# First FFN product of a hybrid encoder step: gate products by VectorE out of PSUM in place, operand sums for the second product by GpSimd

## The chip, the core and the metric

The kernel runs on one core of a Trainium2 chip. A core has a matrix engine (PE in the profile, with its weight loads as PEld), VectorE (DVE), ScalarE (ACT), GpSimd (POOL) and SyncE (SP), which issues most of the DMAs. Every engine works through its own queue in program order and waits at an instruction until the semaphores of that instruction allow it. PE writes its results into PSUM (eight banks of 512 float32 columns on 128 partitions); VectorE and ScalarE read and write PSUM and SBUF; GpSimd works on SBUF here. The metric is the time on the device in microseconds (us); lower is better.

## What is computed

The step runs a two-layer encoder on 1024 prompt frames and 64 sample frames, 1088 columns in all. Layer 0 is an SSD mixer followed by a SwiGLU FFN, layer 1 is band attention followed by a SwiGLU FFN. The change lies in the FFN, which runs once in each layer:

```
def swiglu(u, w_in, w_out):
    g, up = jnp.split(u @ w_in, 2, axis=-1)
    return (jax.nn.silu(g) * up) @ w_out
...
xp = xp + rmsnorm(swiglu(rmsnorm(xp, nw[2]), ffn_w_in[layer], ffn_w_out[layer]), nw[3])
```

The model width is 1024, and the FFN is 2816 wide (22 tiles of 128). Everything is float32; each float32 operand is split into a high part and a low part (`h`, `l_`), and three matmuls (high by high, high by low, low by high) make one product.

## The kernel before

**Layout.** Activations lie transposed: model width on the partitions, frames on the columns. The 1088 columns are cut into two blocks, b=0 with 512 columns and b=1 with 576, and each block into two halves of n=256 or n=288 columns.

**First FFN product.** `back` runs the FFN of one layer. For 6 of the 22 tiles block 0 is computed plainly by `plain_pairs` (`T_PLAIN`): one product for the gate, one for the up part. All other work goes through `run_pair`, which computes gate and up tile of both halves of a block by a scheme of seven products instead of eight (Strassen's in Winograd's form). The products are P1, P6, P2, P7, P5, P4, P3 in this order, each 12 matmuls of 128x128 by 128xn (lines 1389 to 1391). First come 16 pairs with both blocks (`T_BOTH`, tiles k and k+11 in turn for k = 3 to 10), where each product runs for b=0 and then for b=1, except in the very first pair, which runs all of b=0 and then all of b=1; then 6 pairs with block 1 alone (`T_TAIL`: tiles 0, 1, 2, 11, 12, 13). A tile below 11 is called a first-half tile here, and a tile from 11 on a second-half tile (`kh` in `hidden`).

**PSUM.** P1 goes to a bank of a pool of two (`mm`), the other six products take turns on a pool of four banks (`px`). A product can start only when the product four places before it in `px` has been read out. With both blocks, P7 of b=0 takes the bank of P6 of b=0, P5 that of P2, P4 that of P7, P3 that of P5, and the next pair's P6 that of P4. With one block P4 takes the bank of P6, and the next pair's P2 the bank of P5.

**Reading out.** ScalarE copies P1 to `p1` (line 1401). VectorE adds P6 to it as `u2` (1404), P2 into `p1` (1406), and ScalarE takes silu there (1407): the gate of the first half. P7 gives `u3` (1410), P5 gives `c22` and a new `u2` (1413, 1414): `c22` is the up part of the second half. P4 is added into `u3` (1416), ScalarE takes silu (1417), and GpSimd multiplies it by `c22` (1418). P3 is added into `u2` (1420), and GpSimd multiplies `p1` by it into `c22` (1421). For b=1 there is one `p1` buffer, for b=0 there are two; so the copy of P1 of block 1 waits until the multiply of line 1421 of the pair before has read `p1`.

**Operand sums.** `hidden` receives the two finished hidden tiles of a block, stores them to DRAM for the second FFN product (line 1449, issued by SP) and makes the sums that the second product's seven products need (`total`, line 1455): one sum for a first-half tile, three for a second-half tile. All of them run on VectorE. With 22 tiles and 2 blocks in 2 layers that is 176 sums, 24 of them behind `plain_pairs`.

**Weights.** `Weights.pair` prepares the weights of a pair: GpSimd makes two differences (`tt`, lines 317 and 318), VectorE two sums (335, 336), ScalarE and VectorE split them into high and low (371, 372), and GpSimd the low part of the smallest one (`half`, 372). There are three buffers for split weights (`hl`).

**Beside it.** `w2_sums` makes sums of the second product's weights on VectorE (`wsum`, lines 1333 to 1336), tied to PE's progress. In the tail, `loader` and `parted` fetch the first operands of the second product from DRAM and split them on ScalarE and VectorE (lines 1492, 1493).

**What sets the order.** PE's order is written by hand. The other engines' queues are ordered by the scheduler from priorities (`tc.high_priority(HIP)` around everything that reads out a bank) and from its own estimate of times; SP's queue is ordered in the same way.

Of the kernel before, what the change touches and what calls it, by code (L numbers as in the profile page):

```python
# [11 lines left out]
AF = mybir.ActivationFunctionType  # L12
ALU = mybir.AluOpType
# [394 lines left out]
def hybrid_kernel(  # L408
# [5 lines left out]
    V, A, G, PE = nc.vector, nc.scalar, nc.gpsimd, nc.tensor  # L414
# [956 lines left out]
    def run_pair(t_, pr, bs, ends, ops, hid, px, tmp, apart=False, keep=None):  # L1371


        tb = {b: {} for b in bs}
        for (p_, key, c0, i), b in [(x, b) for b in bs for x in PRODS] if apart else [(x, b) for x in PRODS for b in bs]:
            h, v = pr[key]
            n, x = ops[b].n, tb[b]

            def t_new(tag):
                if tag == "u3" and keep is not None:  # L1380
                    return keep[:, t_ * n:(t_ + 1) * n]
                return tmp.tile([P, n], F32, tag=f"{tag}{b}", bufs=2 if tag == "u3" or (tag == "p1" and not b) else 1, name=tag)

            st.wait_for(lambda: i in ops[b].hl)
            ah, al = ops[b].hl[i]
            ps = (px.tile([P, 512], F32, tag="mm", name="px") if p_ != P1 else mm("px"))[:, :n]
            for k in range(4):
                wh, wl = h[:, c0 + k * P:c0 + (k + 1) * P], v[:, c0 + k * P:c0 + (k + 1) * P]
                PE.matmul(ps, wh, ah[:, k, :], start=(k == 0), stop=False)  # L1389
                PE.matmul(ps, wh, al[:, k, :], start=False, stop=False)  # L1390
                at_pe[0] = PE.matmul(ps, wl, ah[:, k, :], start=False, stop=(k == 3))  # L1391
                if k == 1:
                    st.run(6 * n / MMR)
            st.t += 6 * n / MMR
            if b in ends:
                for r in ops[b].rings[i]:
                    r.put()
            with tc.high_priority(HIP):
                if p_ == P1:
                    x["p1"] = t_new("p1")  # L1400
                    A.copy(x["p1"], ps)
                elif p_ == P6:
                    x["u2"] = t_new("u2")
                    V.tensor_tensor(x["u2"], ps, x["p1"], op=ALU.add)  # L1404
                elif p_ == P2:
                    V.tensor_tensor(x["p1"], ps, x["p1"], op=ALU.add)
                    A.activation(x["p1"], x["p1"], AF.Silu)
                elif p_ == P7:
                    x["u3"] = t_new("u3")
                    V.tensor_tensor(x["u3"], ps, x["u2"], op=ALU.add)  # L1410
                elif p_ == P5:
                    x["c22"] = t_new("c22")
                    V.tensor_tensor(x["c22"], ps, x["u3"], op=ALU.add)
                    V.tensor_tensor(x["u2"], ps, x["u2"], op=ALU.add)
                elif p_ == P4:
                    V.tensor_tensor(x["u3"], ps, x["u3"], op=ALU.add)
                    A.activation(x["u3"], x["u3"], AF.Silu)
                    G.tensor_tensor(x["u3"], x["u3"], x["c22"], op=ALU.mult)
                else:
                    V.tensor_tensor(x["u2"], ps, x["u2"], op=ALU.add)  # L1420
                    G.tensor_tensor(x["c22"], x["p1"], x["u2"], op=ALU.mult)
                    hid(t_, b, x["c22"], x["u3"])
            st.pump()
            if p_ in (P2, P7, P4, P3) and b == bs[-1]:
                W.put(p_ == P3)
# [3 lines left out]
    def back(layer, start, cpost, xsrc, xmid, cpre, cpost2, xout, rb_out, done2):  # L1429
# [3 lines left out]
        with ExitStack() as es:  # L1433
# [6 lines left out]
            def hidden(t_, b, x, z, late=None):  # L1440

                kh, k = divmod(t_, KH)
                n = ops[b].n

                def out(i, t):
                    st.spawn(store(i, t), HST)

                def store(i, t):
                    paced(nc.sync.dma_start(hc[:, i, k, HO[b]:HO[b] + n], t))
                    stored[i, b] = stored.get((i, b), 0) + 1  # L1450
                    return
                    yield

                def total(t, x_, y_, op):
                    V.tensor_tensor(t, x_, y_, op=op)
                    return t

                if not kh:
                    s3 = stage[0]()[:, :n] if late is None else late[:, k * n:(k + 1) * n]
                    out(OPI["a11"], x)  # L1460
                    out(OPI["s3"], total(s3, x, z, ALU.subtract))
                    kept[k, b] = z, s3
                    return
                z0, s3 = kept.pop((k, b))
                out(OPI["a12"], x)
                out(OPI["a22"], z)
                out(OPI["s1"], total(z0, z0, z, ALU.add))
                s2 = total(stage[0]()[:, :n], z, s3, ALU.subtract)
                out(OPI["s2"], s2)
                out(OPI["s4"], total(stage[0]()[:, :n], x, s2, ALU.subtract))  # L1470
# [810 lines left out]
```

## Time and profile before

| what | value |
|---|---|
| three runs, us | 2959.5, 2962.66, 2964.96 (median 2962.66) |
| the profiled execution: time and span, us | 2964.38 and 2962.7 |
| TensorE clock granted in it, mean | 0.991 |
| DRAM traffic over the span | 141 GB/s |
| first FFN product with `run_pair`, layer 0 | from about 916 to about 1352 us |
| the same, layer 1 | from about 2280 to about 2717 us |

The page cuts the span into 40 equal slices of 74 us and gives each engine's busy share as a digit in tenths; PEclk is the clock that was granted to TensorE. The two FFNs lie in slices 12 to 21 and 31 to 40.

```profile
PE   8999999999999999999998999999999999999998
DVE  7887878885867776776578778777688777677457
POOL 1333333321022433440021000000131333333012
PEclk9999999999999999999998999999999999999999
```

PE is filled almost everywhere, and GpSimd least. A busy PE can still be a slow PE: the rows for a matmul overlap, and at a lower clock they only become longer.

### The profile page before, as it was taken

To read this page: it belongs to the slowest core of one execution; us is meant where nothing else is said; L and a number is where in the kernel's file an instruction comes from. 1 tells how busy PE (TensorE), PEld (TensorE's weight loads), DVE (VectorE), ACT (ScalarE), POOL (GpSimd) and SP (SyncE) were. 2 spreads that over 40 slices of the span, in tenths; PEclk is the share of its full clock that TensorE was granted. 3 is DMA by queue.
4 is the path that set the end of the run, shared out by engine and by line. 5 is a ranking of instruction groups with operands and counts; after the bars stand their busy time and mean duration, and the time that the engine had idled before them with its cause. 6 is when DMAs were issued, how large, how long until landed. Compare 5 with 4: busy or idle time off the path is not lost. (4 is left out here: it accounts for less than half of the span.)

```text
span 2962.7 us, 58034 instructions
## 1 busy us (share of the span) xinstructions
PE 2864.9 (97%) x22096; PEld 2813.5 (95%) x22096; DVE 2221.4 (75%) x4847; ACT 1367.5 (46%) x2485; POOL 714.1 (24%) x903
## 2 busy tenths in 40 slices
PE   8999999999999999999998999999999999999998
PEld 8999999999999999999997899999999999989998
DVE  7887878885867776776578778777688777677457
ACT  6655545454544222234345566556664222234342
POOL 1333333321022433440021000000131333333012
PEclk9999999999999999999998999999999999999999
DMA  4433333335475454456554222223366445465655
GB/s 137 123 99 100 108 100 106 100 120 179 142 207 145 147 168 156 157 178 214 188 185 148 80 76 78 66 66 91 125 206 190 157 149 166 158 193 183 192 186 166
DMA packets 281479, 424.75 MB, mean 143 GB/s; under 512 B 25328, under 2 KB 231120, under 8 KB 281200
## 3 DMA queue, kind: packets, MB, share of 16 engines
q1 hardware_dynamic: 277968, 410.49, 43.6%
q0 software_dynamic: 3232, 10.56, 2.0%
q8 instruction: 173, 2.83, 0.4%
q14 instruction: 106, 0.87, 0.1%
HBM read 312.30 MB, written 104.19 MB: 141 GB/s over the span
## 5 line engine op out<-in xcount | busy, mean ns | idle before, releaser
L504 PE MATMUL mm<-r,hl 128*128 128x384 f32 (+2 forms) x1704 | 568.3, 334 | 2.7 <-DVE kf L1833 1.2
L506 PE MATMUL mm<-r,hl 128*128 128x384 f32 (+2 forms) x1704 | 551.7, 324 | 5.2 <-DVE hl L385 3.4
L505 PE MATMUL mm<-r,hl 128*128 128x384 f32 (+2 forms) x1704 | 551.3, 324 | 0.0
L1390 PE MATMUL px<-r,hl 128*128 128x288 f32 (+1 forms) x1184 | 350.9, 296 | 0.0
L1389 PE MATMUL px<-r,hl 128*128 128x288 f32 x1056 | 314.9, 298 | 19.3 <-DVE u L1404 8.7
L506 PEld LDWEIGHTS mm<-r,hl 128*128 128x128 f32 x1704 | 322.5, 189 | 6.2 <-DVE hl L385 3.8
L504 PEld LDWEIGHTS mm<-r,hl 128*128 128x128 f32 x1704 | 323.3, 190 | 5.0 <-DVE kf L1833 1.4
L505 PEld LDWEIGHTS mm<-r,hl 128*128 128x128 f32 x1704 | 323.1, 190 | 0.3
L1391 PE MATMUL px<-r,hl 128*128 128x288 f32 x1056 | 314.9, 298 | 0.0
L372 DVE TENSOR_TENSOR hl<-raw,hl 128x1024 fp32r<-128x1024 f32 (+2 forms) x188 | 208.2, 1110 | 141.4 <-ACT hl L371 141.3
L530 POOL TENSOR_TENSOR ssum<-ssum,sq 128x256 f32<-128x256 f32 (+1 forms) x111 | 123.2, 1111 | 573.2 <-ACT sq L529 553.4
L1389 PE MATMUL px<-rx,hl 128*128 128x256 f32 x768 | 217.5, 283 | 24.6 <-DVE u L1404 22.9
L371 ACT CAST hl<-raw 128x1024 fp32r<-128x1024 f32 (+2 forms) x188 | 178.9, 951 | 124.0 <-PE po L1729 86.2
L1390 PEld LDWEIGHTS px<-r,hl 128*128 128x128 f32 x1184 | 225.9, 191 | 0.0
L1389 PEld LDWEIGHTS px<-r,hl 128*128 128x128 f32 x1056 | 201.9, 191 | 22.3 <-DVE u L1404 10.3
L1391 PE MATMUL px<-rx,hl 128*128 128x256 f32 x768 | 214.8, 280 | 3.7 <-DVE hl L372 3.7
L1391 PEld LDWEIGHTS px<-r,hl 128*128 128x128 f32 x1056 | 202.1, 191 | 0.2 <-DVE hl L372 0.2
L1727 PE MATMUL po<-r,hl 128*128 128x288 f32 (+1 forms) x682 | 196.6, 288 | 0.0
L1728 PE MATMUL po<-r,hl 128*128 128x288 f32 (+1 forms) x682 | 196.4, 288 | 0.0
L1729 PE MATMUL po<-r,hl 128*128 128x288 f32 (+1 forms) x682 | 196.4, 288 | 0.0
L1390 PE MATMUL px<-rx,hl 128*128 128x256 f32 x640 | 178.7, 279 | 0.0
L1389 PEld LDWEIGHTS px<-rx,hl 128*128 128x128 f32 x768 | 145.7, 190 | 31.6 <-DVE u L1404 29.9
(433 smaller groups left out, 8301.7 us busy)
## 6 DMA issues: line engine op xcount, KB each, us to landing
raw<-in_w_f_dram SPq DMA_DIRECT2D x104, 512.0 KB, 4.1
wsum<-in_w_f_dram SPq DMA_DIRECT2D x128, 176.0 KB, 3.7
wscr<-wsum SPq DMA_DIRECT2D x128, 176.0 KB, 2.8
raw<-in_w_in_dram SPq DMA_DIRECT2D x40, 512.0 KB, 3.7
MT<-ascr SPq DMA_DIRECT2D x48, 384.0 KB, 4.3
raw<-in_w_so_dram SPq DMA_DIRECT2D x32, 512.0 KB, 4.0
r<-hscr SPq DMA_DIRECT2D x22, 576.0 KB, 5.5
raw<-in_w_o_dram SPq DMA_DIRECT2D x19, 512.0 KB, 3.6
```

The source lines that it names most:

```text
L371: self.nc.scalar.copy(h, v)
L372: (eng or self.eng or self.nc.vector).tensor_tensor(lo, v, h, op=ALU.subtract)
L504: PE.matmul(ps[:, :n], h_, xh, start=(first and i == 0), stop=False)
L505: PE.matmul(ps[:, :n], h_, xl, start=False, stop=False)
L506: PE.matmul(ps[:, :n], l_, xh, start=False, stop=(last and i == nk - 1))
L530: (eng or G).tensor_tensor(ssum[:, :n], ssum[:, :n], q[:, :n], op=ALU.add)
L1389: PE.matmul(ps, wh, ah[:, k, :], start=(k == 0), stop=False)
L1390: PE.matmul(ps, wh, al[:, k, :], start=False, stop=False)
L1391: at_pe[0] = PE.matmul(ps, wl, ah[:, k, :], start=False, stop=(k == 3))
L1727: PE.matmul(ps[:, :n], wh, xh, start=(k == 0), stop=False)
L1728: PE.matmul(ps[:, :n], wh, xl, start=False, stop=False)
L1729: at_pe[0] = PE.matmul(ps[:, :n], wl, xh, start=False, stop=(k == KH - 1))
```

## The change

Three things change in `run_pair` and `hidden`:

- P4 is added to `u3` in its PSUM bank, silu is taken in the bank, and VectorE, no longer GpSimd, multiplies the bank by `c22` into `u3`.
- P3 is added to `u2` in its bank, and VectorE multiplies the bank by `p1` into `c22`.
- The sums of `hidden` (line 1455) run on GpSimd, no longer on VectorE.

```
                 elif p_ == P4:
-                    V.tensor_tensor(x["u3"], ps, x["u3"], op=ALU.add)
-                    A.activation(x["u3"], x["u3"], AF.Silu)
-                    G.tensor_tensor(x["u3"], x["u3"], x["c22"], op=ALU.mult)
+                    V.tensor_tensor(ps, ps, x["u3"], op=ALU.add)
+                    A.activation(ps, ps, AF.Silu)
+                    V.tensor_tensor(x["u3"], ps, x["c22"], op=ALU.mult)
                 else:
-                    V.tensor_tensor(x["u2"], ps, x["u2"], op=ALU.add)
-                    G.tensor_tensor(x["c22"], x["p1"], x["u2"], op=ALU.mult)
+                    V.tensor_tensor(ps, ps, x["u2"], op=ALU.add)
+                    V.tensor_tensor(x["c22"], ps, x["p1"], op=ALU.mult)
                     hid(t_, b, x["c22"], x["u3"])
...
                 def total(t, x_, y_, op):
-                    V.tensor_tensor(t, x_, y_, op=op)
+                    G.tensor_tensor(t, x_, y_, op=op)
                     return t
```

The scheduler then orders the queues anew. PE's queue stays as it was. Three places matter below.

VectorE, end of the first second-half pair with both blocks in layer 0 (tile 14), before the change; `px` is a PSUM bank, `sg` and the `u` with another number on both sides are operand sums:

```order
L335 TENSOR_TENSOR tt<-tt,raw 128x512
L1416 TENSOR_TENSOR u_11608<-px,u_11608 128x256
L1455 TENSOR_TENSOR u_11300<-u_11300,u_11608 128x256
L1455 TENSOR_TENSOR sg<-u_11608,sg 128x256
L1416 TENSOR_TENSOR u_11623<-px,u_11623 128x288
L372 TENSOR_TENSOR hl<-tt,hl 128x1024
L1420 TENSOR_TENSOR u_11539<-px,u_11539 128x256
L1455 TENSOR_TENSOR u_11422<-u_11422,u_11623 128x288
L336 TENSOR_TENSOR tt<-raw,tt 128x512
L1455 TENSOR_TENSOR sg<-c_11653,sg 128x256
L1420 TENSOR_TENSOR u_11556<-px,u_11556 128x288
L1455 TENSOR_TENSOR sg<-u_11623,sg 128x288
```

After one more sum of the same kind come the four `wsum` sums and then line 1404 of the next pair. The same place after the change:

```order
L335 TENSOR_TENSOR tt<-tt,raw 128x512
L1416 TENSOR_TENSOR px<-px,u_11608 128x256
L1418 TENSOR_TENSOR u_11608<-px,c_11653 128x256
L1416 TENSOR_TENSOR px<-px,u_11623 128x288
L372 TENSOR_TENSOR hl<-tt,hl 128x1024
L1418 TENSOR_TENSOR u_11623<-px,c_11669 128x288
L1420 TENSOR_TENSOR px<-px,u_11539 128x256
L336 TENSOR_TENSOR tt<-raw,tt 128x512
L1421 TENSOR_TENSOR c_11653<-px,p_11505 128x256
L1420 TENSOR_TENSOR px<-px,u_11556 128x288
L1421 TENSOR_TENSOR c_11669<-px,p_11524 128x288
L1333 TENSOR_TENSOR wsum<-wsum 128x352
```

The six sums are gone, four multiplies have come in; the first multiply stands straight behind the add whose silu it needs, and the four `wsum` sums and line 1404 follow as before.

GpSimd at the same place, before:

```order
L317 TENSOR_TENSOR tt<-raw 128x512
L1418 TENSOR_TENSOR u_11608<-u_11608,c_11653 128x256
L1418 TENSOR_TENSOR u_11623<-u_11623,c_11669 128x288
L318 TENSOR_TENSOR tt<-raw 128x512
L1421 TENSOR_TENSOR c_11653<-p_11505,u_11539 128x256
L372 TENSOR_TENSOR half<-raw,half 128x512
L1421 TENSOR_TENSOR c_11669<-p_11524,u_11556 128x288
```

And after:

```order
L317 TENSOR_TENSOR tt<-raw 128x512
L1455 TENSOR_TENSOR u_11300<-u_11300,u_11608 128x256
L1455 TENSOR_TENSOR sg<-u_11608,sg 128x256
L318 TENSOR_TENSOR tt<-raw 128x512
L1455 TENSOR_TENSOR u_11422<-u_11422,u_11623 128x288
L372 TENSOR_TENSOR half<-raw,half 128x512
L1455 TENSOR_TENSOR sg<-c_11653,sg 128x256
L1455 TENSOR_TENSOR sg<-u_11623,sg 128x288
L1455 TENSOR_TENSOR sg<-c_11669,sg 128x288
```

Four multiplies have become six sums, two of them ahead of the weights' difference of line 318. In a first-half pair GpSimd has the lines 317, 318 and 372 first and then two sums.

VectorE in the first pair of the tail of layer 0 (tile 0, block 1 alone), before; line 1493 splits operands of the second product:

```order
L335 TENSOR_TENSOR tt<-tt,raw 128x512
L1493 TENSOR_TENSOR rx<-rx 128x1024 x2
L1413 TENSOR_TENSOR c_15595<-px,rx 128x288
L1414 TENSOR_TENSOR u_15527<-px,u_15527 128x288
L1416 TENSOR_TENSOR rx<-px,rx 128x288
L1420 TENSOR_TENSOR u_15527<-px,u_15527 128x288
L1493 TENSOR_TENSOR rx<-rx 128x768
L1455 TENSOR_TENSOR rx<-c_15595,rx 128x288
L1404 TENSOR_TENSOR u_15676<-px,p_15661 128x288
L372 TENSOR_TENSOR hl<-tt,hl 128x1024
```

And after:

```order
L335 TENSOR_TENSOR tt<-tt,raw 128x512
L1416 TENSOR_TENSOR px<-px,rx 128x288
L1493 TENSOR_TENSOR rx<-rx 128x1024
L1413 TENSOR_TENSOR c_15595<-px,rx 128x288
L1414 TENSOR_TENSOR u_15527<-px,u_15527 128x288
L1418 TENSOR_TENSOR rx<-px,c_15595 128x288
L1420 TENSOR_TENSOR px<-px,u_15527 128x288
L1493 TENSOR_TENSOR rx<-rx 128x1024
L1421 TENSOR_TENSOR c_15595<-px,p_15508 128x288
L1493 TENSOR_TENSOR rx<-rx 128x768
L1404 TENSOR_TENSOR u_15676<-px,p_15661 128x288
L372 TENSOR_TENSOR hl<-tt,hl 128x1024
```

One split now stands ahead of line 1414 instead of two, and three stand ahead of line 372 as before.

## The prediction

> **What bounds the kernel now.** I read the page first, then PE's waits. The page's first part shows each engine's busy time:
>
> ```profile
> PE 2864.9 (97%) x22096; PEld 2813.5 (95%) x22096; DVE 2221.4 (75%) x4847; ACT 1367.5 (46%) x2485; POOL 714.1 (24%) x903
> ```
>
> PE is the bound, so the change is worth what it takes from PE's waits, and nothing else. The view of waits, PE alone, lists them by who ended them:
>
> ```profile
> PE px L1389 <- DVE u L1404: 31.6, 33, 2.4
> ...
> PE px L1389 <- DVE u L1414: 6.1, 2, 3.0
> PE px L1389 <- DVE u L1410: 4.0, 2, 3.0
> ```
>
> All three are a product of `run_pair` that waits for its bank to be read out by VectorE: 41.7 us, the largest sum in the whole list. Why is VectorE late? The timeline of VectorE at the end of the pair of tile 14 tells it (start, duration, instruction, idle before):
>
> ```profile
> 968.98 1.23 DVE L336 TENSOR_TENSOR tt<-raw,tt 128x512 f32<-128x512 f32 x1
> 970.13 1.51 DVE L1455 TENSOR_TENSOR sg<-c,sg 128x256 f32<-128x256 f32 x1
> ...
> 973.07 0.46 DVE L1455 TENSOR_TENSOR sg<-c,sg 128x288 f32<-128x288 f32 x1 [0.70 <-POOL c L1421]
> 973.45 0.52 DVE L1333 TENSOR_TENSOR wsum<-wsum 128x352 f32<-128x352 f32 x1
> ...
> 975.56 0.79 DVE L1404 TENSOR_TENSOR u<-px,p 128x256 f32<-128x256 f32 x2
> ```
>
> GpSimd and PE in the same stretch:
>
> ```profile
> 960.91 1.28 POOL L317 TENSOR_TENSOR tt<-raw 128x512 f32<-128x512 f32 x1 [9.97 <-DMA raw<-in_w_f_dram]
> 963.79 0.73 POOL L1418 TENSOR_TENSOR u<-u,c 128x256 f32<-128x256 f32 x1 [1.59 <-ACT u L1417]
> ...
> 967.45 1.29 POOL L318 TENSOR_TENSOR tt<-raw 128x512 f32<-128x512 f32 x1
> 968.70 0.95 POOL L1421 TENSOR_TENSOR c<-p,u 128x256 f32<-128x256 f32 x1
> 969.62 1.74 POOL L372 TENSOR_TENSOR half<-raw,half 128x512 fp32r<-128x512 f32 x1
> 972.14 0.90 POOL L1421 TENSOR_TENSOR c<-p,u 128x288 f32<-128x288 f32 x1 [0.78 <-POOL half L372]
> ```
>
> ```profile
> 974.79 0.29 PE L1391 MATMUL px<-r,hl 128*128 128x288 f32 x1
> 976.03 0.39 PE L1389 MATMUL px<-rx,hl 128*128 128x256 f32 x1 [0.95 <-DVE u L1404]
> ```
>
> GpSimd ends the pair's last multiply at 973.04, because a weight difference of 1.74 us stands ahead of it. VectorE's last sum waits for that; four `wsum` sums follow (973.45 to 975.56), then line 1404, whose first half frees the bank at about 975.98. PE was ready at 975.08. Over the pairs with both blocks, VectorE's own waits name the same cause:
>
> ```profile
> DVE sg L1455 <- POOL c L1421: 28.6, 23, 2.0
> ```
>
> A long wait costs more than itself. Two of them in PE's timeline, and then the windows behind the five longest, with the granted clock in the third column from the right:
>
> ```profile
> 1291.75 0.61 PE L1389 MATMUL px<-r,hl 128*128 128x288 f32 x1 [3.04 <-DVE u L1414]
> 1335.85 0.61 PE L1389 MATMUL px<-r,hl 128*128 128x288 f32 x1 [2.43 <-DVE u L1404]
> ```
>
> ```profile
> 1292.00:1298.00 6.00, 6.00 (x26) 6.00 (x27) 4.43 (x8) 2.27 (x5) 3.18 (x3) 0.50 0.70 242
> 1336.00:1340.00 4.00, 4.00 (x21) 4.00 (x22) 4.00 (x6) 2.21 (x3) 0.00 (x0) 0.63 0.33 87
> 2656.00:2662.00 6.00, 6.00 (x34) 5.81 (x34) 4.43 (x8) 2.49 (x5) 3.15 (x3) 0.72 0.57 181
> 2700.00:2704.00 4.00, 4.00 (x20) 4.00 (x21) 4.00 (x6) 2.33 (x3) 0.00 (x0) 0.60 0.38 103
> 2297.00:2303.00 6.00, 5.49 (x30) 5.50 (x31) 3.43 (x9) 0.90 (x2) 1.47 (x2) 0.72 0.67 210
> ```
>
> What is missing to 1.0 is lost: 6x0.50 + 4x0.37 + 6x0.28 + 4x0.40 + 6x0.28 = 9.4 us. The ceiling of the gain from these waits is 41.7 + 9.4 = 51.1 us.
>
> **The multiplies.** GpSimd loses 152 of them (lines 1418, 1421) and VectorE gets them:
>
> ```profile
> L1418 POOL TENSOR_TENSOR u<-u,c 128x288 f32<-128x288 f32 x18 | 23.8, 1322 | 27.4 <-ACT u L1417 27.4
> L1421 POOL TENSOR_TENSOR c<-p,u 128x288 f32<-128x288 f32 x21 | 18.2, 866 | 11.9 <-POOL half L372 11.7
> L1420 DVE TENSOR_TENSOR u<-px,u 128x288 f32<-128x288 f32 x21 | 9.4, 446 | 0.0
> ```
>
> One bank operand and one SBUF operand take VectorE 446 ns, against 866 to 1322 on GpSimd. No row here has VectorE write a bank; its nearest rows are line 1420 (446 ns) and the longest sum below (1533 ns), and I take 0.45. Even at 1.5 VectorE has room: with both blocks it is busy 238 of 337 us (the row below), and per layer 76 multiplies at 0.45 are 34 us while 76 sums leave it.
>
> ```profile
> 935.00:1272.00 337.00, 325.28 (x2589) 321.76 (x2588) 238.41 (x415) 92.16 (x156) 122.75 (x107) 1.00 0.50 161
> ```
>
> The multiply of line 1418 adds a wait: VectorE stands still from the end of the add until ScalarE's silu is done. Queued behind it are the next block's add, a weight split and line 1420. The silu costs:
>
> ```profile
> L371 ACT CAST hl<-tt 128x1024 fp32r<-128x1024 f32 x42 | 43.8, 1042 | 20.2 <-PE px L1391 20.1
> ...
> L1417 ACT ACTIVATE u<-u 128x288 f32<-128x288 f32 x18 | 8.0, 443 | 12.1 <-DVE u L1416 12.1
> ```
>
> ScalarE already waits for that add, so the stall is about 0.5 us, once per pair with both blocks (for block 1 the split of 1.2 us covers it). Bounds: 0.4, and 1.5 when a cast of 1.04 us is in ScalarE's way. The bank of P4 is held for 0.9 us longer (silu and multiply), that of P3 for 0.45; each has four products until its next use, and a product of 12 matmuls takes 12 x 337/2589 = 1.56 us, so over 5 us: no cost.
>
> **The sums.** VectorE loses 176, GpSimd gets them. Here they took:
>
> ```profile
> L1455 DVE TENSOR_TENSOR u<-u,u 128x288 f32<-128x288 f32 x8 | 12.3, 1533 | 2.9 <-POOL u L1418 2.9
> L1455 DVE TENSOR_TENSOR sg<-c,u 128x288 f32<-128x288 f32 x8 | 3.7, 458 | 8.8 <-POOL c L1421 8.8
> ```
>
> The same work takes 458 ns, or 1533 where a GpSimd instruction runs beside it. Line 1420, with one SBUF input, shows no such spread. The page SBUF — State Buffer of the Trainium skill (Who interferes with whom) has a rule that speaks against this change: a VectorE instruction with two SBUF inputs and a GpSimd instruction that reads SBUF exclude each other for their whole length, so each sum moved to GpSimd can hold up the weight splits and `wsum` sums that stay on VectorE. The two rows agree with it; what it would make of the time is the first rival.
>
> On GpSimd I take 0.85 us a sum (line 1421; bounds 0.73 and 1.5), so six are 5.1 us in place of four multiplies of some 4 us; a pair of 14 products lasts 14 x 1.56 = 22 us, so GpSimd keeps room.
>
> **Pairs with both blocks.** In the pair above, the first multiply can begin when GpSimd's did, at 963.79, and ends at about 964.2. Two sums, 1.7 to 3.0 us, then line 318 (1.29) give 967.2 to 968.5; before it was 968.74. Then VectorE: line 336 1.23, lines 1421, 1420, 1421 1.3, four `wsum` sums 2.1, line 1404 0.42, together 5.1 us: the bank is free between 972.3 and 973.6, and PE needs it at 975.1. The slack is 1.5 to 2.8 us. In first-half pairs no sum stands ahead of line 318, so the slack is larger. The waits for line 1404 end in these pairs.
>
> **The first pair.** Line 1410 waits for a buffer whose store follows a sum:
>
> ```profile
> 923.02 0.42 DVE L1363 TENSOR_TENSOR x<-mmx,x 128x256 f32<-128x256 f32 x1
> ...
> 926.09 1.66 DVE L336 TENSOR_TENSOR tt<-raw,tt 128x512 f32<-128x512 f32 x1
> ...
> 933.78 0.42 DVE L1410 TENSOR_TENSOR u<-px,u 128x256 f32<-128x256 f32 x1 [4.57 <-DMA hscr<-x]
> ```
>
> VectorE made that sum only behind the weight sum of line 336, so after 927.75. Its inputs were there at 923.44 (line 1363), and on GpSimd nothing but a DMA issue stands ahead, so the store leaves some 4 us earlier and the 4.0 us of PE waits go.
>
> **The tail.** The 3.0 us wait for line 1414 comes from two splits ahead of it:
>
> ```profile
> 1287.54 3.42 DVE L1493 TENSOR_TENSOR rx<-rx 128x1024 fp32r<-128x1024 f32 x2
> 1290.88 0.45 DVE L1413 TENSOR_TENSOR c<-px,rx 128x288 f32<-128x288 f32 x1
> ...
> 1295.66 1.22 DVE L372 TENSOR_TENSOR hl<-tt,hl 128x1024 fp32r<-128x1024 f32 x1
> ```
>
> After, one split stands ahead, and VectorE arrives 2.2 us earlier: it has lost two sums of 1.53 and two of 0.46 and gained four multiplies of 0.45. From 1285.3 an add, one split (1.2 to 2.3) and two read-outs free P5's bank at 1287.9 to 1289.0. PE wanted it at 1288.7, and without two waits of the mean 0.96 (31.6/33) ahead of it at 1286.8: 1 to 2 us are left. Behind it two splits (2.1 to 3.2), four read-outs and multiplies (1.8) and the weight split itself (1.22 at 1295.66 before) still follow, 5.1 to 6.2 us, which ends at 1293 to 1295; PE wants these weights two products after its wait, at 1291.7: 1.5 to 3.5 us. I take 4 us a layer for both. The wait of 2.43 at 1335.85 loses two sums of 1.53 and one of 0.46 from its chain: nothing is left of it.
>
> New waits: 2 x 4 = 8 us. With the clock that they cost, by the rows of 0.50 to 0.72 about 1 us each, 2 us more. By the page TensorE: Matmul & The Clock Gate of the Trainium skill (Part 1) the clock falls only after an idle window of about 3.4 us, so these waits would cost nothing more and the gain were 43.1; the wait of 2.43 us with 0.63 behind it says otherwise.
>
> **The sum.** 51.1 - 8 - 2 = 41.1 us. The profiled execution took 2964.38 us (span 2962.7), which gives 2923.3; it lies 1.7 above the median of 2962.66, from which I get 2921.6, rounded 2922.
>
> **The rivals.**
>
> *Half.* GpSimd's sums run while VectorE does the `wsum` sums and weight splits, all with two SBUF inputs. In second-half pairs three sums meet four `wsum` sums. One that did so took 1.13:
>
> ```profile
> 1279.17 1.13 DVE L1333 TENSOR_TENSOR wsum<-wsum 128x352 f32<-128x352 f32 x1
> ```
>
> If each of the four does, 2.4 us are added, and up to 1 us on the splits: more than the slack of 1.5. For: the 1533 ns row. Against: GpSimd was busy there before, too. Price: a wait of about 1.4 us in the 16 second-half pairs, 22 us: 2944. This is what the rule of the Trainium skill's page SBUF — State Buffer comes to here.
>
> *No gain.* The stall at silu and the longer banks take the place of the waits, one for one. Over 44 pairs 41.1 us is 0.9 us each, on top of the slack of 1.5: VectorE would have to lose 2.4 us in each; the worst bound of the stall is 1.5. 2963.
>
> *Slower.* Place: line 318 behind two sums. If line 318 comes later than 967.2 by more than 2.8 us, every us beyond is PE's; over 16 second-half pairs it eats the 41.1 us at 2.6 us more, so it decides from 5.4 us of lateness. GpSimd's raw weights arriving late (its 9.97 us wait before line 317 in this pair) plus sums at 1.5 could do it. At 7 us: 16 x 4.2 = 67, less 41.1, gives 2989. Against: the multiplies stood at the same place before.
>
> *More.* The tail's new waits do not come: 2962.7 - 51.1 = 2912. VectorE also has 12 sums less a layer around the first pair, 12 x 0.46 = 5.5 us, of which half may reach PE: 2906.
>
> **How the numbers follow.** Forecast (gain 30 to 51) 0.61, half 0.18, more 0.07, no gain 0.06, slower 0.08. The range takes in the first three: 2906 to 2950 (half with a bad tail), leaving out about 0.17. Faster by over 0.2% (5.9 us, about what a measurement of this kernel tells from no change) 0.86, within 0.06, slower 0.08.
>
> **What would show it.** Right: PE's waits for line 1404 fall from 31.6 to under 5 us, the one for 1410 goes, VectorE's waits for GpSimd's line 1421 are gone, and in the tail PE waits for line 372. Half: rows of `wsum` near 1.1 us and waits for 1404 in every second pair. Wrong: VectorE's wait for line 318, or for silu, in microseconds per pair.

## The result and the profile after

The changed kernel takes 2917.52 us (median of 4 runs, 2915.51 to 2922.25), beside 2963.81 us for the kernel before on the same chip: ratio 0.9847, 95% interval 0.983 to 0.9865. That is 46 us less, where the prediction had 41 (2922, range 2906 to 2950). The profiled execution has a span of 2916.6 us, 46.1 less than before.

The first part of the page after:

```profile
PE 2850.9 (98%) x22096; PEld 2806.7 (96%) x22096; DVE 2237.3 (77%) x4823; ACT 1367.2 (47%) x2485; POOL 753.1 (26%) x927
```

VectorE and GpSimd are both busier than before (2221.4 and 714.1 us), and the kernel is faster. The view of waits, PE alone, its largest lines for products of `run_pair` (line waited for: us in total, times, longest):

```profile
PE px L1391 <- DVE hl L372: 5.9, 5, 2.4
PE px L1389 <- DVE u L1414: 4.7, 3, 2.5
PE px L1389 <- DVE u L1410: 2.8, 1, 2.8
```

Four more lines, 1363, 1406, 371 and 1418, have one wait each, 1.9 us together. Of the 5.9 us for line 372, 5.6 lie in the first pairs and only 0.3 in a tail. Line 1404, 31.6 us in 33 waits before, is gone. VectorE's own waits show why: no line is left in which it waits for GpSimd's line 1421, nor for any multiply or sum. It waits for silu, as expected, and longer than before for stores:

```profile
DVE u L1418 <- ACT px L1417: 13.0, 30, 0.4
DVE c L1413 <- DMA hscr<-c: 10.4, 7, 2.8
DVE u L1410 <- DMA hscr<-x: 8.7, 2, 6.3
```

VectorE at the end of the pair of tile 14, the place that the prediction worked through:

```profile
965.33 1.78 DVE L336 TENSOR_TENSOR tt<-raw,tt 128x512 f32<-128x512 f32 x1
...
967.85 0.46 DVE L1421 TENSOR_TENSOR c<-px,p 128x288 f32<-128x288 f32 x1
968.22 1.18 DVE L1333 TENSOR_TENSOR wsum<-wsum 128x352 f32<-128x352 f32 x1
...
971.47 1.01 DVE L1336 TENSOR_TENSOR wsum<-wsum 128x352 f32<-128x352 f32 x1
972.40 0.78 DVE L1404 TENSOR_TENSOR u<-px,p 128x256 f32<-128x256 f32 x2
```

GpSimd and PE there:

```profile
965.27 1.29 POOL L318 TENSOR_TENSOR tt<-raw 128x512 f32<-128x512 f32 x1
...
968.98 1.02 POOL L1455 TENSOR_TENSOR sg<-c,sg 128x256 f32<-128x256 f32 x1
...
971.13 0.97 POOL L1455 TENSOR_TENSOR sg<-c,sg 128x288 f32<-128x288 f32 x1
```

```profile
973.95 0.28 PE L1389 MATMUL px<-rx,hl 128*128 128x256 f32 x1
```

Three sums run on GpSimd beside the four `wsum` sums, and these last from 968.22 to 972.48, 4.26 us, where they took 2.11 before. The sign of the rival *Half* is there in full, but its price is not: line 1404's first half ends at 972.81 and PE takes the bank at 973.95, without a wait. 1.14 us of room are left.

### The profile page after: what moved, and what is told of

It is laid out like the page before. It is cut to its first block, busy times and chain, and to the rows that moved or that the text cites. A ratio compares the mean times of both kernels' runs of the same rounds, so it can differ in the third digit from the quotient of the medians.

```text
span 2916.6 us, 57887 instructions
## 1 busy us (share of the span) xinstructions
PE 2850.9 (98%) x22096; PEld 2806.7 (96%) x22096; DVE 2237.3 (77%) x4823; ACT 1367.2 (47%) x2485; POOL 753.1 (26%) x927
## 4 chain that ended last, share of the span: by engine, by line
PE 81%; DVE 10%; DMA 4%; ACT 2%; issue 2%; SPq 0%; POOL 0%; DVEq 0%; ACTq 0%; POOLq 0%
PE px L1390 8%; PE px L1391 8%; PE px L1389 8%; PE mm L504 8%; PE mm L506 8%; PE mm L505 8%; PE po L1729 4%; PE po L1728 4%; PE po L1727 4%; PE mmx L505 3%; PE mmx L506 3%; PE mmx L504 3%; PE ptp L1955 2%; PE po L1990 2%; PE S L1924 1%
## 5 line engine op out<-in xcount | busy, mean ns | idle before, releaser
L372 DVE TENSOR_TENSOR hl<-raw,hl 128x1024 fp32r<-128x1024 f32 (+2 forms) x188 | 214.1, 1141 | 125.5 <-ACT hl L371 125.4
```

The lines of the kernel that those rows point to most:

```text
L372: (eng or self.eng or self.nc.vector).tensor_tensor(lo, v, h, op=ALU.subtract)
```

## The experiments

Each kernel was timed beside the kernel before on one chip; ratios are against that. Where times lie close, I also give the length of the two stages (first to last matmul of lines 1389 to 1391, both layers together): 871.1 us before, 826.8 after. What lies between the stages is untouched, yet it differs between profiles by up to 7 us (923.9 to 930.9). Every edit also makes the scheduler order the queues anew, so a run shows a move together with its new order.

**Which of the moves makes the gain?** First the multiplies alone, then the sums alone:

```diff
 def total(t, x_, y_, op):
-    G.tensor_tensor(t, x_, y_, op=op)
+    V.tensor_tensor(t, x_, y_, op=op)
```

> Half of the change: the multiplies of lines 1418 and 1421 on VectorE out of the banks, the sums of line 1455 left on VectorE. My theory (the waits came from VectorE's last sum waiting for GpSimd's multiply; after the change the pairs that hold second-half tiles have 0.8 to 1.3 us to spare at line 1404, the others 1.8 to 2.8): VectorE's waits for GpSimd's line 1421 (55.5 us before) are gone, and the wsum sums are back at 0.52 us (from 1.1) because GpSimd does no sums beside them, which gives 2.1 us back per second-half pair; but six sums of 0.46 to 1.5 us now stand ahead of them, 2.8 us and more. Net some 1 to 2 us later than in the changed kernel, against 0.8 to 1.3 to spare: waits of 0 to 1 us for line 1404 in the 16 to 22 second-half pairs, none in the others: 2918 + 0 to 20, I say 2928. Rival (taking the multiplies off GpSimd is the whole gain, where the sums run does not matter): 2918, no waits for line 1404.

Measured: 2912.44 us, ratio 0.983 (0.9815 to 0.9845), stages 825.0. That is all of the gain, and my theory was too dark by 16 us. VectorE in the same pair, and the product of PE that takes the bank:

```profile
966.11 0.51 DVE L1333 TENSOR_TENSOR wsum<-wsum 128x352 f32<-128x352 f32 x1
...
966.91 0.51 DVE L1334 TENSOR_TENSOR wsum<-wsum 128x352 f32<-128x352 f32 x1
967.35 0.68 DVE L336 TENSOR_TENSOR tt<-raw,tt 128x512 f32<-128x512 f32 x1
967.95 0.51 DVE L1335 TENSOR_TENSOR wsum<-wsum 128x352 f32<-128x352 f32 x1
968.39 0.41 DVE L1404 TENSOR_TENSOR u<-px,p 128x256 f32<-128x256 f32 x1
```

```profile
971.35 0.28 PE L1389 MATMUL px<-rx,hl 128*128 128x256 f32 x1
```

The room is 971.35 - 968.80 = 2.55 us, more than with the sums on GpSimd; 0.51 of it comes from the order, since line 1404 now stands ahead of the last `wsum` sum. VectorE makes six sums more, but with GpSimd quiet its `wsum` sums fall back to 0.51 us and line 336 to 0.68. Two windows of the same length in the stage with both blocks (here, then the changed kernel; behind the window's length stand the busy times of PE, weight loads, VectorE, ScalarE and GpSimd, then the granted clock) show that moving the sums off VectorE freed nothing on it, 244.3 us against 247.9:

```profile
935.00:1255.00 320.00, 320.00 (x2574) 320.00 (x2574) 244.30 (x471) 93.64 (x156) 64.99 (x46) 1.00 0.52 168
```

```profile
935.00:1255.00 320.00, 320.00 (x2574) 320.00 (x2573) 247.90 (x415) 91.66 (x155) 124.96 (x104) 1.00 0.52 170
```

The sums alone, with the multiplies on GpSimd as before:

> The other half: the sums of line 1455 on GpSimd, the multiplies left on GpSimd as before. My theory: VectorE no longer waits for GpSimd (wait for line 1421 gone), but GpSimd's last multiply is now behind three or four sums of about 1 us, so it ends 3 to 4 us later than before; ScalarE's copy of line 1401 for the second block waits for it (it has one p1 buffer), and line 1404 for that copy. The wait moves from VectorE's sum to ScalarE's copy and is of the same size: PE's waits for line 1404 10 to 40 us, time 2945 (2925 to 2970). Rival (the waits came from VectorE standing at the sum and from nothing else): no waits for line 1404 above 5 us in all, 2918 to 2922.

Measured: 3018.2 us, ratio 1.0188 (1.0171 to 1.0205): 56 us slower, and 48 us above the end of the range that my theory gave. The move of the sums is a loss by itself. PE's waits, VectorE's and ScalarE's:

```profile
PE px L1389 <- DVE u L1404: 66.8, 36, 6.2
```

```profile
DVE tt L335 <- POOL tt L317: 96.8, 41, 5.1
DVE u L1404 <- ACT p L1401: 95.8, 41, 3.8
```

```profile
ACT p L1401 <- POOL c L1421: 290.9, 41, 10.0
```

The copy of line 1401 waits as expected (192.1 us in 41 waits before), but it is not all. GpSimd and SyncE in this kernel, from the pair of tile 14 on:

```profile
973.92 1.28 POOL L372 TENSOR_TENSOR half<-raw,half 128x512 fp32r<-128x512 f32 x1
...
988.20 1.29 POOL L317 TENSOR_TENSOR tt<-raw 128x512 f32<-128x512 f32 x1 [11.35 <-DMA raw<-in_w_f_dram]
```

```profile
975.24 0.33 SPq L279 DMA_DIRECT2D raw<-in_w_f_dram  x1
```

The half split ends at 975.20 (971.36 before). It is the last reader of a weight buffer, so SyncE issues the next weight load right behind it, and everything of the next pair's weights comes some 4 us later: line 335 begins at 989.53, before at 985.41. This I had not named, and it hits the first-half pairs, which I had called safe: in layer 0 the eight of them end in 15.3 us of waits for line 1404, the eight second-half pairs in 12.9.

**Which multiply?** From the kernel with the multiplies moved and the sums left, line 1418 goes back to GpSimd (with silu and add in SBUF), or line 1421 does:

```diff
-V.tensor_tensor(ps, ps, x["u3"], op=ALU.add)
-A.activation(ps, ps, AF.Silu)
-V.tensor_tensor(x["u3"], ps, x["c22"], op=ALU.mult)
+V.tensor_tensor(x["u3"], ps, x["u3"], op=ALU.add)
+A.activation(x["u3"], x["u3"], AF.Silu)
+G.tensor_tensor(x["u3"], x["u3"], x["c22"], op=ALU.mult)
```

> One of the two multiplies alone: line 1421 (product P3, the last of a pair) on VectorE out of the bank; line 1418 stays on GpSimd, the sums on VectorE. With both multiplies moved and the sums left, the time was 2912 and line 1404 had 2.5 to 2.9 us to spare. Theory A (what was late is GpSimd's last multiply of a pair, line 1421, as the prediction has it): with it gone nearly all of the gain is there. VectorE's sum behind line 1418 still waits up to 1.3 us and line 318 comes about 1.3 us later, which the room covers: 2912 to 2922, I say 2916, under 8 us of waits for line 1404. Theory B (each hand-over between VectorE and GpSimd in a pair costs its share): about half, 2937, 15 us of waits.

```diff
-V.tensor_tensor(ps, ps, x["u2"], op=ALU.add)
-V.tensor_tensor(x["c22"], ps, x["p1"], op=ALU.mult)
+V.tensor_tensor(x["u2"], ps, x["u2"], op=ALU.add)
+G.tensor_tensor(x["c22"], x["p1"], x["u2"], op=ALU.mult)
```

> The other multiply alone: line 1418 (product P4, with silu in the bank) on VectorE; line 1421 stays on GpSimd, behind line 318 and half a weight split, the sums on VectorE. Theory A (line 1421 being behind the half split is the cause): VectorE's waits for GpSimd's line 1421 stay, and with them most of PE's waits for line 1404: 20 to 30 us of them, 2945 to 2960. Theory B (each hand-over has its share): without line 1418, GpSimd comes to line 318 several us sooner, its last multiply ends some 2 to 4 us sooner, and 1 to 1.5 us of room are left at line 1404: 2914 to 2925, I say 2920. I hold B for the likelier one for this run.

Measured: line 1421 alone 2922.43, ratio 0.9861 (0.9843 to 0.9879), stages 830.8; line 1418 alone 2934.37, ratio 0.9899 (0.9877 to 0.9921), stages 845.8. So the last multiply of the pair is worth 39 us of the 50 by itself, at the upper end of what theory A had, with 2.2 us of waits for line 1404 left, all in the tails. But line 1418 by itself is worth 27, which neither theory gave: A had 2945 to 2960, and B, which I held for the likelier one, 2914 to 2925. GpSimd, without line 1418, comes to its last multiply sooner (in the pair of tile 14 it ends at 971.71, before at 973.04). The two overlap. With line 1418 alone moved, VectorE's sums into `sg` keep 32.5 of the 55.5 us that they waited for line 1421 over both layers before, and little room is left:

```profile
DVE sg L1455 <- POOL c L1421: 32.5, 48, 2.0
```

```profile
PE px L1389 <- DVE u L1404: 8.7, 9, 1.7
```

**What is the bank worth?** Both multiplies on VectorE with two SBUF inputs, silu and adds in SBUF as before. First with the sums on GpSimd, then with the sums on VectorE:

```diff
-G.tensor_tensor(x["u3"], x["u3"], x["c22"], op=ALU.mult)
+V.tensor_tensor(x["u3"], x["u3"], x["c22"], op=ALU.mult)
-G.tensor_tensor(x["c22"], x["p1"], x["u2"], op=ALU.mult)
+V.tensor_tensor(x["c22"], x["p1"], x["u2"], op=ALU.mult)
```

> The change without the banks: both multiplies on VectorE and the sums on GpSimd, but line 1416 and line 1420 write to SBUF as before, silu stays in SBUF, and the multiplies have two SBUF inputs. My theory (VectorE instructions with two SBUF inputs and GpSimd's sums hold each other up, those with a bank input don't): the rows of lines 1418 and 1421, 0.44 us and never over 0.46 in the changed kernel, show means of 0.55 to 0.9 with longest ones over 1 us; GpSimd's sums beside them get slower too; some 0.5 to 1.5 us of VectorE time per pair, against 0.8 to 1.3 to spare in second-half pairs: 2918 to 2930, I say 2922. Rival (the place of the operand does not matter): rows of 0.45, 2918.

> Only the engine of both multiplies is changed: they run on VectorE with two SBUF inputs, silu and both adds stay in SBUF as before, the sums stay on VectorE. Against the run with the same sums and the multiplies out of the banks (2912), it shows what the banks are worth while GpSimd does no sums. Theory (two SBUF inputs cost only where a GpSimd instruction runs beside them; with the sums on GpSimd line 1421 took 1.03 us that way and the time was 2930): GpSimd is quiet but for line 318 and the half split, so the row of line 1421 shows 0.45 to 0.75 us, and the room of 2.5 to 2.9 us covers it: 2912 to 2917, no waits for line 1404. Rival (the bank is worth its 12 us in itself, by freeing or reading it): 2924 or more.

Measured: 2929.82, ratio 0.9888 (0.9873 to 0.9902), stages 842.5, with the sums on GpSimd; 2918.1, ratio 0.9845 (0.9825 to 0.9865), stages 828.0, with the sums on VectorE. The row of line 1421 in the changed kernel, then in these two (shortest, median and longest of its instructions, in ns):

```profile
L1421 DVE TENSOR_TENSOR c<-px,p x76: 409/445/459, 936.5 to 2673.5; 128x288 f32<-128x288 f32 x44, 128x256 f32<-128x256 f32 x32
```

```profile
L1421 DVE TENSOR_TENSOR c<-p,u x76: 426/1028/1571, 934.2 to 2684.4; 128x288 f32<-128x288 f32 x44, 128x256 f32<-128x256 f32 x32
```

```profile
L1421 DVE TENSOR_TENSOR c<-p,u x76: 425/451/1570, 932.1 to 2672.5; 128x288 f32<-128x288 f32 x44, 128x256 f32<-128x256 f32 x32
```

Out of the bank no instruction of 76 took over 0.46 us, though 72 of them ran beside a GpSimd instruction. From SBUF it takes that only where GpSimd is quiet: in the last of these kernels 38 of the 76 ran beside a GpSimd instruction, and 36 of these took over 0.6 us; none of the other 38 took over 0.455. The bank is worth 12 us in the kernel with the sums on GpSimd; with the sums on VectorE a worth between 0 and 5 us cannot be told from nothing, since the intervals of 0.9845 and 0.983 overlap.

**How much room is there at line 1404?** In the changed kernel, the last multiply of each pair made five times:

```diff
-V.tensor_tensor(x["c22"], ps, x["p1"], op=ALU.mult)
+for _ in range(5 if b == bs[-1] else 1):
+    V.tensor_tensor(x["c22"], ps, x["p1"], op=ALU.mult)
```

> The changed kernel with the last multiply of each pair (line 1421 of its last block) made five times, 4 x 0.45 = 1.8 us of VectorE more ahead of the wsum sums and line 1404. It measures the room at line 1404. Theory (the contention took 2.1 us of a room of 3 in second-half pairs and left 0.8 to 1.3; 1.8 to 2.8 in first-half pairs): waits for line 1404 of 0.5 to 1.0 us come back in some 16 to 22 second-half pairs, none in the first-half ones: 12 to 20 us of waits, time 2932. Rival (the room is wider than that, since VectorE was idle at other points and catches up): under 5 us of waits, under 2924.

Measured: 2955.52, ratio 0.9973 (0.9962 to 0.9985). It did not measure what it was made for. The repeats were interleaved with the `wsum` sums, the last of which fell behind line 1404, and in the pairs with both blocks PE hardly waits (0.9 us for line 1404 in layer 0, 1.0 in layer 1). The time was lost in the tails, where the five multiplies, with weight splits between them, held the bank of product P3 for 6 us longer (the loop makes the code a line longer, so line 1422 is this multiply):

```profile
PE px L1389 <- DVE c L1422: 28.1, 8, 5.8
```

What it does show: a bank held some 6 us longer is no longer free of cost. The 0.45 and 0.9 us of the change cost PE one wait of 0.4 us (line 1418). The room at line 1404 stays unmeasured.

**The tail.** A second buffer for c22 of the second block, in the changed kernel:

```diff
-bufs=2 if tag == "u3" or (tag == "p1" and not b) else 1
+bufs=2 if tag == "u3" or (tag == "c22" and b) or (tag == "p1" and not b) else 1
```

> The changed kernel with a second buffer for c22 of the second block. In the changed kernel's tail VectorE stands at line 1413 until the store of an earlier c has landed (10.4 us in 7 waits, 3.9 in 2 before), because that store left SyncE behind stores of sums that GpSimd had not made yet; PE then waits for line 1414 (4.7 us). Theory (the store behind GpSimd's sums is what ends the tail's wait): VectorE's waits for stores of c fall from 10.4 to under 2 us, PE's for line 1414 from 4.7 to under 2, with the clock 3 to 5 us in all: 2913. Rival (VectorE arrives at that place late anyway, for the splits of line 1493): PE's wait for line 1414 or for line 372 stays at 4 us or more, 2917.

Measured: 2916.01, ratio 0.9838 (0.9818 to 0.9858), stages 824.8. VectorE's waits for stores of c are gone, and PE's for line 1414 fall from 4.7 to 0.2. But line 372 takes their place, 2.5 us in the first tail and 2.4 in the second:

```profile
PE px L1391 <- DVE hl L372: 10.1, 6, 2.5
```

The theory was right about the store and wrong about the time. With the store's wait gone, a wait of the same size stands behind the three splits of line 1493 that VectorE makes ahead of line 372, as the rival had it.

**The first pair.** In the changed kernel, two of the last tile's three sums of the first stage go back to VectorE; only s1, for whose store I took line 1410 to wait, stays on GpSimd:

```diff
-def total(t, x_, y_, op):
-    G.tensor_tensor(t, x_, y_, op=op)
+def total(t, x_, y_, op, last=False):
+    (V if last and not b and t_ == T_PLAIN[-1] else G).tensor_tensor(t, x_, y_, op=op)
...
-s2 = total(stage[0]()[:, :n], z, s3, ALU.subtract)
+s2 = total(stage[0]()[:, :n], z, s3, ALU.subtract, True)
...
-out(OPI["s4"], total(stage[0]()[:, :n], x, s2, ALU.subtract))
+out(OPI["s4"], total(stage[0]()[:, :n], x, s2, ALU.subtract, True))
```

> The changed kernel with two of the three sums of the last tile of the first stage back on VectorE; the one whose store line 1410 waits for stays on GpSimd. Theory (three sums of 1.4 to 1.7 us each on GpSimd hold up line 318 there, SyncE's weight load waits for line 318, and the store stands behind that load): the load leaves some 2 us sooner, VectorE's waits at line 1410 for a store fall from 8.7 to under 6 us, PE's from 2.8 to under 1: 2914. Rival (the store's own landing or VectorE's splits end that wait): 2.8 us stay, 2917.

Measured: 2916.11, ratio 0.9843 (0.9822 to 0.9865), stages 822.6. VectorE's wait at line 1410 for the store falls from 8.7 to 5.1 us, as expected, PE's only from 2.8 to 2.4 (1.5 and 0.9 in the two layers), where I had expected under 1. The stages are 4 us shorter, but that is the clock: PE's waits in them are 15.7 us, 15.3 in the changed kernel, while the granted clock was 1.00 where there it was 0.93 for 26 us (2255 to 2281) and 0.72 for 6 us (from 2615). The whole time cannot be told from the changed kernel's.

**A faster kernel?** The multiplies out of the banks, all sums on VectorE but that one; and the same with a split of the tail on GpSimd:

```diff
-out(OPI["s1"], total(z0, z0, z, ALU.add))
+out(OPI["s1"], total(z0, z0, z, ALU.add, G if not b and t_ == T_PLAIN[-1] else V))
```

> A try at a faster kernel, and a test of the first pair: both multiplies on VectorE out of the banks, all sums on VectorE but one, the sum of the last tile of the first stage whose store line 1410 of the first pair waits for; that one is on GpSimd. Theory (on VectorE that sum stands behind weight splits, in the second layer until 2264.9, while SyncE is ready for its store at 2259.9; on GpSimd it is done 7 us sooner and ahead of line 318, so neither line 318 nor SyncE's queue is held up; with all three sums of that tile on GpSimd, as in the changed kernel, line 318 came 2 us late, SyncE's weight load waited for it, and the stores stood behind that load): PE's wait for line 1410 in the second layer (2.4 us) goes, in the first layer it stays, since there the store's landing ends it: 2.5 to 4.5 us less than with all sums on VectorE, 2909. Rival (the transfer is slow because of the four weight loads beside it, whenever it starts): the waits stay, 2912.

```diff
-paced(V.tensor_tensor(rr(l_), l_, rr(h_), op=ALU.subtract))
+paced((G if (p_, b) == USE[0] and k == 4 else V).tensor_tensor(rr(l_), l_, rr(h_), op=ALU.subtract))
```

> A try at a faster kernel: both multiplies on VectorE out of the banks, all sums on VectorE but the one of the first pair (its run was 2912), and the second of the three splits of line 1493 in each tail on GpSimd, which is idle there. Theory (in the tail PE waits 2.1 us a layer for line 372, and VectorE makes that split 1.2 us behind one of line 1493 of 1.2 to 2.3 us): the two waits fall below 1 us each, 3 to 5 us less: 2908. Rival (on GpSimd the split takes 2.5 us and more, beside VectorE's own two-input splits, and holds up the half split of line 372): the waits move to the half split's product or stay: 2912.

Measured: the first 2912.54, ratio 0.983 (0.9809 to 0.9852), with the shortest stages of all, 819.7; PE's wait for line 1410 is down to 0.3 us over both layers, where I had expected it to stay in the first; yet the time is the rival's 2912, not 2909. The second 2914.99, ratio 0.9834 (0.9815 to 0.9854), stages 821.6: its waits in the tails moved back from line 372 to line 1414 (2.1 and 2.9 us). The rival was right here, by VectorE's sum of line 335, which took 0.69 us in the first tail of the changed kernel (at 1269.42). VectorE, then GpSimd:

```profile
1267.20 2.88 DVE L335 TENSOR_TENSOR tt<-tt,raw 128x512 f32<-128x512 f32 x1 [1.43 <-POOL tt L317]
```

```profile
1267.12 2.41 POOL L1493 TENSOR_TENSOR rx<-rx 128x1024 fp32r<-128x1024 f32 x1
```

Neither is proved faster than the plain move of the multiplies.

**The changed kernel again:**

> The changed kernel itself, unaltered, beside the three above on the same chip. It is to say how much of the 5 us between it (2917.5) and the kernel with the sums left on VectorE (2912.4) is its own spread: the two stages that the change touches differ by 1.8 us only in the two profiles (826.8 against 825.0 us), the rest lies in stretches that neither touches. If the sums on GpSimd do cost 5 us, this run comes out at 2916 to 2919; if the difference is spread, at 2911 to 2915.

Measured: 2918.47, ratio 0.9845 (0.9825 to 0.9866), stages 827.5. Both times that it was run, the changed kernel came out 5 to 6 us above the two kernels with the sums left on VectorE (2912.44, 2912.54), 4 to 5 by the ratios. All these intervals overlap, so I take it as likely, not shown, that the sums on GpSimd cost some 5 us. The traces don't show where: PE's waits in the stages are 15.3 and 15.6 us in the two profiles of the changed kernel, and 15.5 with all sums on VectorE.

## Why the prediction was right, step by step

**The bound and the cause.** Right. PE's waits for line 1404 went from 31.6 us to nothing, with VectorE's waits for line 1421. That the multiplies did it is shown by the first two experiments; the prediction had counted sums and multiplies as one move, and so credited the sums with a part that they do not have.

**The multiplies.** 0.45 us was right (409 to 459 ns), the silu stall too: 13.0 us in 30 waits, 0.43 each, against 0.5. The longer hold of the banks cost next to nothing, one wait of 0.4 us.

**The sums.** 0.85 us was too low: the changed kernel's medians by operands lie between 0.81 and 1.72 us, and nine of the ten are 0.95 or more. That VectorE gains what its sums leave free was wrong: in the window above it is 3.6 us busier with them gone. The `wsum` sums show it best, in the changed kernel and with the sums on VectorE: medians of 1.146 and 0.510 us. The rule of the Trainium skill's page SBUF — State Buffer (Who interferes with whom), that a VectorE instruction with two SBUF inputs and a GpSimd instruction that reads SBUF exclude each other, agrees with these rows.

```profile
L1333 DVE TENSOR_TENSOR wsum<-wsum x32: 508/1146/1245, 948.4 to 2602.6; 128x352 f32<-128x352 f32 x32
```

```profile
L1333 DVE TENSOR_TENSOR wsum<-wsum x32: 506/510/1248, 945.8 to 2595.6; 128x352 f32<-128x352 f32 x32
```

**Pairs with both blocks.** The result was right, the working had a wrong link. (Its "weight difference of 1.74 us" is the half split of line 372.) I let line 336 follow line 318. It doesn't wait for it: in the profile after it starts at 965.33, 0.06 us after line 318 starts. VectorE thus came to the `wsum` sums earlier than I had it, and that paid for *Half*: its 2.15 us were taken out of a room of 1.14 + 2.15 = 3.3 us, where I had given it 1.5 to 2.8 and had judged *Half* by the 1.5. *Slower*, which hung on line 318, had no path to line 1404 through line 336 either.

**The first pair.** Wrong: of the 4.0 us for line 1410, 2.8 stayed. The step was "on GpSimd nothing but a DMA issue stands ahead, so the store leaves some 4 us earlier". The sum was early, the stores not. GpSimd and SyncE there:

```profile
923.38 1.70 POOL L1455 TENSOR_TENSOR x<-x 128x256 f32<-128x256 f32 x1 [2.11 <-issue]
925.05 2.85 POOL L1455 TENSOR_TENSOR sg<-x,sg 128x256 f32<-128x256 f32 x2
927.85 1.28 POOL L318 TENSOR_TENSOR tt<-raw 128x512 f32<-128x512 f32 x1
```

```profile
912.25 17.25 SPq L279 DMA_DIRECT2D raw<-in_w_f_dram  x2
929.58 0.80 SPq L1449 DMA_DIRECT2D hscr<-x  x1
```

The sum ends at 925.08. But the tile's three stores stand in SyncE's queue behind a weight load that needs the buffer which line 318 reads, and line 318 now stands behind three sums of 1.4 to 1.7 us, until 929.13. The stores leave from 929.58 on; before, they left from 927.65. I had looked at the queue of the engine that makes the sum, not at the one that issues its store.

The step has a second fault: the store that line 1410 waits for here is not the sum's. It is the second of the three, which waits for VectorE's result and not for GpSimd's sum. It is issued at 930.47 and lands 3.4 us later; line 1410 starts at 933.95, when the third (issued at 930.90, 3.3 us) has not landed. Before, it was the second as well (issued at 928.13, 5.6 us to landing, line 1410 at 933.78).

That PE's wait of 1.05 us for line 1410 in layer 0 went is no gain either. VectorE reads that bank 18.4 us after the stage's start, before 17.1; PE came late itself, after a wait of 2.36 us for line 372 (1.37 before) and at a clock of 0.50. All waits of the first pairs together are 10.5 us, before 9.9. With only the one sum ahead of line 318 VectorE's wait went down (the run for the first pair), and with it and GpSimd otherwise free PE's went to 0.3 us.

**The tail.** The forecast was 8 us of new waits; 4.8 came, 4.5 of them at another line (2.5 and 2.0 for line 1414, 0.3 for line 372). I had line 372 behind the splits; in the changed kernel line 1414 comes first:

```profile
1273.32 0.46 DVE L1413 TENSOR_TENSOR c<-px,rx 128x288 f32<-128x288 f32 x1 [1.71 <-DMA hscr<-c]
```

```profile
1265.32 1.51 SPq L1449 DMA_DIRECT2D hscr<-sg  x2
1266.93 0.40 SPq L1449 DMA_DIRECT2D hscr<-c  x1
```

The store of c left at 1266.93, behind two stores of sums that GpSimd makes until 1265.41, and landed as VectorE went on at 1273.32. With a second buffer that wait goes, and the forecast wait for line 372 stands in its place, 2.5 and 2.4 us.

**The sum.** Forecast and measurement agree better than their parts, and that is luck. All of PE's waits in the two stages fell from 48.0 us (the three lines in the prediction and 6.3 us of four smaller ones) to 15.3: 32.7 less, against 33.7 forecast. By place they fell from 22.9 to 0 in the pairs with both blocks and from 15.2 to 4.8 in the tails, and rose by 0.6 in the first pairs. The clock was forecast to give 7.4 back. By the rows of before (first pair and tail of each layer: 0.91 for 19 us, 0.94 for 80, 0.93 for 23, 0.96 for 81; with both blocks 1.00) 11.4 us were lost, and after, by these rows, 3.4 + 1.4 + 1.8 + 1.4 = 8.0 us:

```profile
915.00:934.00 19.00, 14.78 (x98) 14.20 (x98) 11.85 (x14) 6.87 (x9) 7.85 (x6) 0.82 0.35 99
...
1256.00:1328.00 72.00, 69.50 (x515) 69.18 (x515) 61.58 (x90) 31.89 (x47) 38.05 (x29) 0.98 0.59 183
2255.00:2281.00 26.00, 19.71 (x137) 18.23 (x136) 23.53 (x28) 13.63 (x18) 9.74 (x7) 0.93 0.33 90
...
2600.00:2669.00 69.00, 66.73 (x492) 66.27 (x491) 59.43 (x87) 30.56 (x44) 34.25 (x28) 0.98 0.61 191
```

So 3.4 us from the clock, not 7.4. What made up for it is a term that I left out. In the wait of 0.95 us quoted in the prediction, PE's matmul of 974.79 lasts 0.29 us, yet matmuls follow each other 0.13 us apart; the next one started 1.24 us after it, so 1.24 - 0.13 = 1.11 us were lost, 0.16 more than the row of the wait says. The matmul behind the wait, at 976.03, is slow as well; the one after it starts 0.23 us later, and 0.12 is usual:

```profile
976.26 0.28 PE L1390 MATMUL px<-r,hl 128*128 128x256 f32 x1
```

With 43 waits before and 13 after, an estimate from this one wait is 30 x (0.16 + 0.11) = 8.1 us. 32.7 + 3.4 + 8.1 = 44.2 of the 44.3 us by which the stages got shorter (871.1 to 826.8); so close a sum is chance, for the rounding of the clock column alone (0.005 of 827 us) is 4 us. 1.8 us lie outside the stages.

## What to carry to other kernels

When two engines hand work back and forth, take the last step of the chain off the engine whose queue holds other work, and leave the rest alone: here the multiplies were the whole gain, and the sums that went the other way gave VectorE no time back, because instructions of two SBUF inputs ran longest where GpSimd worked. One input in a PSUM bank kept an instruction out of that. And a result is only as early as the queue that stores it: follow each moved step to the engine that issues its DMA.

## What the runs showed of the hardware

- VectorE with two SBUF inputs beside GpSimd: 0.51 became 0.94 to 1.25 us (`wsum`), 0.68 became 1.78 (line 336). With one input in a bank the longest of 76 was 0.459.
- Writing its result into the bank cost VectorE next to nothing: line 1416 takes 455 ns so in the median, 448 before. Silu in the bank is a little faster on ScalarE, 394 ns against 443 (128x288).
- A wait of PE costs more than its idle time in the trace: in the one worked out above 0.16 us, the overlap of two matmuls, and 0.11 us for a slow first matmul.
- The granted clock was 0.74 in the 6 us behind a wait of 2.50 us (1274.20), and 0.50 behind one of 2.36 us (926.22); yet it was 1.00 behind the wait of 2.79 us at 2274.91. In the second run of the same kernel, the same wait, 2.80 us at 2273.57, had 0.50 from 2273 to 2279. So the length of a wait does not decide alone; what does stays open. The page TensorE: Matmul & The Clock Gate of the Trainium skill (Part 1) has the clock fall after an idle window of about 3.4 us; the falls behind 2.36 to 2.80 us of waiting do not agree with it.
- A fall can be short: in the changed kernel the clock was 1.00 from 1270.0 to 1273.6, 0.50 from 1273.7 to 1277.0, and 1.00 again from 1277.2. The 0.74 is the mean over both states.
